# Every third weight tile's remainder computed by GpSimd in place of VectorE, in a one-core decoder layer in float32

## The chip, the cores and the metric

The kernel runs on one NeuronCore of a Trainium2 chip. Its engines work side by side and meet at semaphores: PE multiplies matrices, DVE (VectorE), ACT (ScalarE) and POOL (GpSimd) work on tiles in the on-chip memory SBUF, SP issues the loads and stores. Products land in PSUM. The metric is the device time of one execution in microseconds (us).

## The reference

One decoder layer on x of 256 tokens by 2048 channels, float32 throughout. Three sub-layers, each wrapped in two RMS norms and a shift, a scale and a gate that come from a conditioning vector c:

```python
mod = (silu(c) @ w_ada + b_ada)                      # 2048 -> 9 rows of 2048
h = rms_norm(x, g_pre) * (1 + scale) + shift
x = x + coef * gate * rms_norm(fn(h), g_post)
# fn: FFN 0, mixer, FFN 1
ffn(h) = (silu(h @ w_gate) * (h @ w_up)) @ w_down    # 2048 -> 5632 -> 2048
mixer(h): proj = h @ w_in; mLSTM heads and a spatial gate; concat @ w_out
```

Nearly all the time goes into products of 256 tokens with large weights, each of which is read from memory once.

## The kernel before, in words

A weight is taken in tiles of 256 rows by 512 columns (128 partitions x 1024 values; 410 or 412 columns in part of the mixer). For each tile, `load_w` (L271) issues a 512 KB load into one of eight `raw` buffers (`rawp`, L50), and `split_w` (L277) splits it in two: ACT casts `raw` to the rounded copy `wh` (L284), DVE subtracts, `wl = raw - wh`, the remainder (L285). Both are of the type float32r, and together they hold the weight exactly. They live in one of `NW = 4` buffers each (`wsp`, L51), or, for a few tiles kept across a sub-layer's end, in other memory ("slots"). The activations are split likewise into `hh` and `hl`, and `mm3` (L302) makes three products for each pair: hh with wh (L303), hl with wh (L304), hh with wl (L305). In part of the program the operands are swapped, and there it is L304 that takes `wl`. A tile feeds 24 matmuls of 256 columns or 12 of 512.

Beside the weight tiles run the modulation rows: `ada_sums` (L141) loads tiles of `w_ada` into the same eight `raw` buffers, and DVE adds each up with one multiply-add of 128 x 1024 values (L164, `acc`), a step after each weight tile or two. `behind` (L135) orders such an addition after the DVE remainder that was issued last (`last_split`), without a semaphore. The stages are: FFN 0's first part, in which DVE also makes the norms (to about 210 us), the rest of FFN 0 (to 800), the mixer (to 1145, with a boundary of norms to 1200), and FFN 1 (to 1890), which has few modulation rows.

The program is written through a tile framework. It gives each engine its own order of instructions, by its estimate of when each could run, and puts the semaphores in. Each engine, and SP's queue of loads, then runs strictly in that order. POOL has 40 small instructions in this kernel, among them the power -1/2 of the norms: `rstd` (L354), `brs` (L773) and `qv` (L998).

Of the kernel before, what the change touches and what calls it, by code (L numbers as in the profile page):

```python
# [8 lines left out]
F32 = mybir.dt.float32  # L9
# [23 lines left out]
def tile_layer(  # L33
# [42 lines left out]
    class Half:  # L76
        """Half of the tokens in the tile that holds the residual stream between the sub-layers"""

# [13 lines left out]

# [1 line left out]
    ident = cpool.tile([P, P], F32, name="ident")  # L94
# [7 lines left out]

# [1 line left out]
    xt = cpool.tile([P, NT, D], F32, name="xt")  # L104
# [24 lines left out]

# [1 line left out]
    last_split = [None]  # L131
    floor = [None, None]
    last_update = [None]

    def behind(ins, other):  # L135
        """ins is issued after other, on the same engine"""
        if other is not None:
            tc.add_manual_dep(ins.ins, other.ins.name, mybir.DependencyInfo(
                mybir.DependencyClass.NoSync, mybir.DependencyReason.DATA), reason="order")

    def ada_sums(runs, n):  # L141
        """Sums over the rows on each partition of the runs of n columns that start at runs; a step loads a
        tile and adds up the one before. The additions wait for the weight tile that was loaded after."""
        acc = adap.tile([P, 2, 512], F32, tag="acc", name=nm("acc"))
# [24 lines left out]
    def ada_cols(a, r, c0, n):  # L169
        """The sum over the partitions as columns of A or B."""  # L170
        sub, kind = r // 3, r % 3
        m0, m = c0 // P, n // P
        pa = ps()
        for i in range(m):
            nc.tensor.transpose(pa[:, i * P:(i + 1) * P], a[:, i * P:(i + 1) * P], ident)  # L175
        bias = v1[:, r * NK + m0:r * NK + m0 + m]
        dst = (bm if kind == 0 else am)[:, sub, m0:m0 + m]
        nc.vector.tensor_reduce(out=dst, in_=pa[:, 0:n].rearrange("p (m k) -> p m k", k=P), axis=AX.X, op=ALU.add)
        if kind == 0:
            nc.vector.tensor_tensor(out=dst, in0=dst, in1=bias, op=ALU.add)  # L180
        else:
            nc.vector.scalar_tensor_tensor(dst, dst, 1.0, bias, op0=ALU.add, op1=ALU.add)
            gp = v2[:, 16 + sub * NK + m0:16 + sub * NK + m0 + m]
            nc.vector.tensor_tensor(out=dst, in0=dst, in1=gp, op=ALU.mult)

    def ada_row(a, sub, c0):
        """The sum over the partitions as a gate's row on all of them, times g_post."""
        if gg[0] is None:
# [16 lines left out]
    def ada_unit(r, half):  # L205
        """1024 columns of one modulation row"""
        c0 = half * 1024
# [8 lines left out]
    class Side:  # L216
        """Modulation rows computed beside the weight tiles, spread evenly over n_main of them."""

# [25 lines left out]

# [1 line left out]
    pending = []  # L246
# [20 lines left out]

# [1 line left out]
    FULL = [(0, 4, 0), (4, 4, 4), (8, 4, 8), (12, 4, 12)]  # L269
# [7 lines left out]
    def split_w(rawv, slot, w):  # L277
# [6 lines left out]
        behind(nc.scalar.copy(wh, rawv), floor[1])  # L284
        last_split[0] = nc.vector.tensor_tensor(out=wl, in0=rawv, in1=wh.bitcast(F32), op=ALU.subtract)  # L285
        behind(last_split[0], floor[0])
        return wh, wl
# [19 lines left out]
    def hold(src, segs, c0, nw):  # L307
        """All the tiles of segs split and kept, those beyond the first nw halves in the large slots."""
        n = sum(nk for _, nk, _ in segs) // 2
# [3 lines left out]
    def proj_t(src, c0, segs=FULL, banks=None, first=0):  # L313
        """[512 weight columns, S] in two banks, each 2 x [128, S]: the sum over the chunks from first on."""
        banks = banks or [ps(), ps()]
# [11 lines left out]
    def proj_tok(src, c0, begun=None, w=512):  # L327
        """[S, w weight columns] in two banks, one per 128 tokens."""
        banks, done = begun or ([ps(), ps()], 0)
# [8 lines left out]

# [1 line left out]
    def parts():  # L340
        """The means of the squares over a token's quarters, the last one apart; EPS beside the others."""
        p = small((P, 8), "parts")
        nc.gpsimd.memset(p[:, 3:4], EPS)
        return p
# [12 lines left out]
    def modulate(sub, k0, nk, src, n0, n1, act):  # L357
        """h = n * A + B for the 128-channel chunks from k0 on, split into hh, hl."""
        w = n1 - n0
# [21 lines left out]
    def to_h(sub, t, q, n):  # L381
        """Four channel chunks of one half of the tokens, transposed and modulated."""
        for i in range(0, 4, 2):
# [6 lines left out]
    def pre_norm_q(sub, q, rs, act=False):  # L390
        """Four channel chunks of all the tokens."""
        modulate_q(sub, q, transposed_q(q, rs), act)
# [16 lines left out]
    def post_norm_t(y, t, r, z, last, xin):  # L409
        """x += GG * y * rstd(y) for one half of the tokens"""  # L410
        z3 = z(t)
# [18 lines left out]
    def early_w(src, c0, w):  # L430
        """The first weight tiles of the next sub-layer, split ahead into the part of hh and hl that is written
        last."""
        if src is None:
# [9 lines left out]
    def boundary(last_mm, evac, times_g, xin, y, yp, free, early, ahead, nxt, src=None, c0=None, w=512):  # L443
        """The last products of a sub-layer, one half of the tokens after the other, the residual, and the
        next sub-layer's h with the first products that take it, the first half's beside the second half's
        norms."""
        kept = [] if nxt is None else early + list(w_tiles(src, [(4, 2 * ahead, 4)], c0, w=w))
# [49 lines left out]

# [1 line left out]
    def swiglu_evac(g, gb, ub):  # L499
# [8 lines left out]
    def swiglu_sum(gb, ub, part):  # L508
        """The same after the sums over the first chunks, in part, have been added; the result takes its place."""
        pv = part.t.rearrange("p k s -> p (k s)")  # L510
# [15 lines left out]
    def swiglu_tok(g, gb, ub):  # L526
        """The same from products that have the tokens on the partitions."""
        gts = []
# [16 lines left out]
    def ffn(idx, supers, begun, xin, nxt, nxt_src=None, nxt_c0=None, nxt_w=512):  # L545
        """supers: lists of (block, chunk tiles that are left, sums over the others in SBUF or in PSUM)"""
        y = None
# [69 lines left out]

    # ================= FFN 0 =================
    # The first blocks run over the channel chunks that are modulated so far: five over the first four, three over
    # eight, and one over twelve, which stays in PSUM.  # L620
    gate_up = (w_ff_gate[0], w_ff_up[0])
    rs = [x_sumsq(t) for t in range(NT)]

    def ada_pair(c0, n):
        """A and B of the first sub-layer for n channels"""
        for acc in ada_sums((D + c0, c0), n):
# [22 lines left out]
    class First:  # L649
        """The rest of the first sub-layer's modulation beside the first weight tiles."""  # L650

# [49 lines left out]
    class Reload:  # L701
        """The residual stream again: its tile takes the products' sums."""

# [19 lines left out]

    # ================= mixer =================
    mix_side = Side([(5, 0), (5, 1), (7, 0), (7, 1)], 1)
# [27 lines left out]

    # gv, u and the gates from the last 2056 columns, gv first
    gv = Slot((P, NT, DM))
# [7 lines left out]
    def gated_norm(t):  # L763
        """layer norm of gelu(gv)"""
        st = small((P, 2, 6), "bst")
# [45 lines left out]
    def gates():  # L811
        """The stabilised gate weights: with a_s = i_s - cumsum(log f)_s and the running maximum M_l of a
        (and of the state's), pp holds exp(a_s - M_l) under the causal mask for chunk pairs (0, 0), (0, 1)
        and (1, 1); em holds exp(-m_l)."""
        nc.vector.scalar_tensor_tensor(ea, gx[:, :, 4:8], -1.0, gx[:, :, 4:8], op0=ALU.mult, op1=ALU.max)
# [72 lines left out]
    def spatial():  # L888
        """z = gelu(u) * (W v + b), into the second half of the concatenation"""
        for i in range(2):  # L890
# [76 lines left out]

    # o: sigmoid, times the head norm's weight
    so = Slot((P, NT, DM))
# [8 lines left out]
    def values():  # L978
        """The weighted sums of the values, and of ones beside them."""
        for h in range(H):  # L980
# [91 lines left out]

    # ================= FFN 1 =================
    side[0] = Side([(8, i) for i in range(2)], 100)
# [31 lines left out]
```

## Time and profile before

| | |
|---|---|
| runs | 1909.9 and 1910.4 us, median 1910.15 |
| profiled execution | span 1910.4 us, which is its time; nothing of note lies around the span |
| PE matmul | 1862.1 us busy, 97% |
| DVE | 1356.0 us, 71% |
| ACT | 855.2 us, 45% |
| POOL | 17.2 us, 1% |
| loads | 500 MB, 262 GB/s on average, 334 GB/s from 40 to 210 us |

Busy times of PE are modelled ends of pipelined matmuls, so a full row says that PE always had work, and no more. The stages differ: a share over the whole span says little about one of them, so the rows further down are taken by stage. A wait row names an engine, what it waited for, the time in total, how often and the longest.

### The profile page before, as it was taken

What the parts mean: (1) busy time and instruction counts of PE and PEld (TensorE: products, weight loads), DVE (VectorE), ACT (ScalarE), POOL (GpSimd) and SP (SyncE); (2) the same over time, 40 slices, a digit from 0 to 9 for tenths busy, and PEclk for the clock granted to TensorE, in tenths of its full rate; (3) what the DMA queues carried; (4) which work ended last, traced back from release to release, by engine and by line L of the source; (5) the groups of instructions that cost most, each with busy time, mean ns of one, the idle gap of its engine ahead of it and who ended that gap; (6) DMA issues with size and microseconds to landing.
All of it is one profiled execution on the core that took longest, in us unless ns stands there. A gap on an engine that the chain in (4) does not pass through costs nothing.

```text
span 1910.4 us, 30740 instructions
## 1 busy us (share of the span) xinstructions
PE 1862.1 (97%) x12357; PEld 1714.0 (90%) x12357; DVE 1356.0 (71%) x1465; ACT 855.2 (45%) x1059; POOL 17.2 (1%) x40
## 2 busy tenths in 40 slices
PE   3999999999999999999999999999999999999998
PEld 2999998899988998799988887999889999899986
DVE  7788788778887878868888986555556555555455
ACT  3545444444443434555545446444444444334443
POOL 0000000000000000000000000000000000000000
PEclk9999999999999999999999999999999999999999
DMA  9999889888898998678688994666666666666552
GB/s 352 344 329 333 285 300 317 303 304 309 299 326 305 357 310 298 207 220 278 230 278 308 354 326 129 217 218 211 227 221 209 220 218 212 220 225 214 187 187 88
DMA packets 232647, 500.31 MB, mean 262 GB/s; under 512 B 16829, under 2 KB 28333, under 8 KB 231993
## 3 DMA queue, kind: packets, MB, share of 16 engines
q1 hardware_dynamic: 232504, 498.36, 76.7%
q8 instruction: 96, 1.57, 0.3%
q14 instruction: 47, 0.38, 0.1%
HBM read 496.19 MB, written 2.10 MB: 261 GB/s over the span
## 4 chain that ended last, share of the span: by engine, by line
PE 89%; issue 8%; DVE 2%; ACT 1%; POOL 1%; DMA 0%; POOLq 0%; DVEq 0%; ACTq 0%
PE ps L303 29%; PE ps L305 29%; PE ps L304 29%; DVE acc L164 1%; PE ps L175 0%; DMA xt<-in_x_dram 0%; PE ps L403 0%; POOL rstd L354 0%; DVE wl L285 0%; ACT t L365 0%; DMA raw<-in_w_in_dram 0%; PE ps L895 0%; ACT t L348 0%; POOL brs L773 0%; ACT hh L336 0%
## 5 line engine op out<-in xcount | busy, mean ns | idle before, releaser
L285 DVE TENSOR_TENSOR wl<-raw,wh 128x1024 fp32r<-128x1024 f32 (+2 forms) x637 | 769.0, 1210 | 488.7 <-ACT wh L284 488.0
L284 ACT CAST wh<-raw 128x1024 fp32r<-128x1024 f32 (+2 forms) x637 | 661.2, 1042 | 882.6 <-PE ps L304 453.5
L303 PE MATMUL ps<-hh,wh 128*128 128x256 f32 x2816 | 794.5, 282 | 3.7 <-ACT hh L336 3.1
L304 PE MATMUL ps<-hl,wh 128*128 128x256 f32 x2816 | 792.2, 281 | 0.0
L305 PE MATMUL ps<-hh,wl 128*128 128x256 f32 x2816 | 791.6, 281 | 0.0
L303 PEld LDWEIGHTS ps<-hh,wh 128*128 128x128 f32 x2816 | 531.7, 189 | 5.4 <-ACT hh L336 3.7
L304 PEld LDWEIGHTS ps<-hl,wh 128*128 128x128 f32 x2816 | 531.9, 189 | 1.1 <-issue 0.5
L305 PEld LDWEIGHTS ps<-hh,wl 128*128 128x128 f32 x2816 | 531.4, 189 | 0.1
L164 DVE SCALAR_TENSOR_TENSOR acc<-raw,cs,acc 128x1024 f32<-128x1024 f32 x270 | 345.1, 1278 | 0.5
L303 PE MATMUL ps<-wh,big 128*128 128x512 f32 x804 | 318.0, 395 | 0.0
L305 PE MATMUL ps<-wh,big 128*128 128x512 f32 x804 | 316.4, 394 | 0.0
L304 PE MATMUL ps<-wl,big 128*128 128x512 f32 x804 | 316.4, 393 | 0.0
L305 PEld LDWEIGHTS ps<-wh,big 128*128 128x128 f32 x804 | 150.9, 188 | 35.8
L303 PEld LDWEIGHTS ps<-wh,big 128*128 128x128 f32 x804 | 151.0, 188 | 34.4
L304 PEld LDWEIGHTS ps<-wl,big 128*128 128x128 f32 x804 | 151.0, 188 | 34.3
L303 PE MATMUL ps<-wh,hh 128*128 128x512 f32 (+2 forms) x336 | 127.2, 380 | 0.0
L304 PE MATMUL ps<-wl,hh 128*128 128x512 f32 (+2 forms) x336 | 126.0, 375 | 0.6 <-DVE wl L285 0.6
L305 PE MATMUL ps<-wh,hl 128*128 128x512 f32 (+2 forms) x336 | 125.7, 374 | 0.0
L304 PEld LDWEIGHTS ps<-wl,hh 128*128 128x128 f32 x336 | 63.2, 188 | 9.3 <-DVE wl L285 1.3
L305 PEld LDWEIGHTS ps<-wh,hl 128*128 128x128 f32 x336 | 63.1, 188 | 8.4
L303 PEld LDWEIGHTS ps<-wh,hh 128*128 128x128 f32 x336 | 63.0, 188 | 8.0 <-ACT hh L336 0.2
L645 ACT COPY big<-ps 128x512 f32<-128x512 f32 x32 | 18.8, 588 | 45.0 <-PE ps L305 43.4
(195 smaller groups left out, 718.2 us busy)
## 6 DMA issues: line engine op xcount, KB each, us to landing
raw<-in_w_ada_dram SPq DMA_DIRECT2D x224, 512.0 KB
raw<-in_w_ff_gate_dram SPq DMA_DIRECT2D x176, 512.0 KB
raw<-in_w_ff_up_dram SPq DMA_DIRECT2D x176, 512.0 KB
raw<-in_w_ff_down_dram SPq DMA_DIRECT2D x176, 512.0 KB
raw<-in_w_ada_dram SPq DMA_DIRECT2D x128, 256.0 KB
raw<-in_w_in_dram SPq DMA_DIRECT2D x48, 512.0 KB
raw<-in_w_out_dram SPq DMA_DIRECT2D x32, 512.0 KB
raw<-in_w_in_dram SPq DMA_DIRECT2D x24, 412.0 KB
```

The costliest lines, as they stand in the source:

```text
L164: ins = nc.vector.scalar_tensor_tensor(a, raw[:, j, :, :], cs[:, k:k + 1], a, op0=ALU.mult, op1=ALU.add)
L284: behind(nc.scalar.copy(wh, rawv), floor[1])
L285: last_split[0] = nc.vector.tensor_tensor(out=wl, in0=rawv, in1=wh.bitcast(F32), op=ALU.subtract)
L303: nc.tensor.matmul(o, lh, rh, start=start, stop=False, skip_group_check=True)
L304: nc.tensor.matmul(o, lh, rl, start=False, stop=False, skip_group_check=True)
L305: nc.tensor.matmul(o, ll, rh, start=False, stop=stop, skip_group_check=True)
L645: nc.scalar.copy(part.t.rearrange("p k s -> p (k s)")[:, u * 1024 + i * 512:u * 1024 + (i + 1) * 512], banks[i])
```

## The change

A counter goes up with each weight tile. At every third count, if the tile lives in the four `wsp` buffers, POOL computes `wl` with the same operation, and `last_split` stays at the DVE remainder before it; the order behind `floor[0]`, which places some remainders after a norm's instruction, isn't set for these either. All else in the diff takes out comments and docstrings, so that lines of the changed file from split_w on stand five further down.

```diff
+    n_split = [0]
...
         behind(nc.scalar.copy(wh, rawv), floor[1])
-        last_split[0] = nc.vector.tensor_tensor(out=wl, in0=rawv, in1=wh.bitcast(F32), op=ALU.subtract)
-        behind(last_split[0], floor[0])
+        n_split[0] += 1
+        if slot is None and n_split[0] % 3 == 0:
+            nc.gpsimd.tensor_tensor(out=wl, in0=rawv, in1=wh.bitcast(F32), op=ALU.subtract)
+        else:
+            last_split[0] = nc.vector.tensor_tensor(out=wl, in0=rawv, in1=wh.bitcast(F32), op=ALU.subtract)
+            behind(last_split[0], floor[0])
         return wh, wl
```

213 remainders move to POOL, of 648. PE's and SP's orders stay nearly as they were; DVE's and POOL's change. Two places are shown. The numbers in the names are the tiles' own, the same before and after.

The first place is DVE at the start of the third modulation pass in FFN 0 (145 to 160 us in the trace of before). Before:

```order
L285 TENSOR_TENSOR wl_1647<-raw_1644,wh_1646 128x1024
L164 SCALAR_TENSOR_TENSOR acc_1602<-raw_1641,cs,acc_1602 128x1024
L337 TENSOR_TENSOR hl<-t_237_1592,hh 128x512
L378 TENSOR_SCALAR t_336_2387<-xt,rstd_125 128x512
L378 TENSOR_SCALAR t_337_2389<-xt,rstd_139 128x512
L285 TENSOR_TENSOR wl_1682<-raw_1679,wh_1681 128x1024
L337 TENSOR_TENSOR hl<-t_238_1597,hh 128x512
L164 SCALAR_TENSOR_TENSOR acc_1602<-raw_1676,cs,acc_1602 128x1024
L285 TENSOR_TENSOR wl_1716<-raw_1713,wh_1715 128x1024
L285 TENSOR_TENSOR wl_1746<-raw_1743,wh_1745 128x1024
```

And now, on the same engine:

```order
L290 TENSOR_TENSOR wl_1647<-raw_1644,wh_1646 128x1024
L165 SCALAR_TENSOR_TENSOR acc_1602<-raw_1641,cs,acc_1602 128x1024
L342 TENSOR_TENSOR hl<-t_237_1592,hh 128x512
L165 SCALAR_TENSOR_TENSOR acc_1602<-raw_1676,cs,acc_1602 128x1024
L342 TENSOR_TENSOR hl<-t_238_1597,hh 128x512
L383 TENSOR_SCALAR t_336_2387<-xt,rstd_125 128x512
L383 TENSOR_SCALAR t_337_2389<-xt,rstd_139 128x512
L290 TENSOR_TENSOR wl_1716<-raw_1713,wh_1715 128x1024
L290 TENSOR_TENSOR wl_1746<-raw_1743,wh_1745 128x1024
```

`wl_1682` has left DVE for POOL, and the addition that stood behind it has moved ahead of a norm's two instructions.

The second place is POOL in the mixer at 1024 us, where `qv` is the power that the head norm needs. Before, nothing but that stood on POOL between 928 and 1143 us. Now:

```order
L288 TENSOR_TENSOR wl_10478<-raw_10475,wh_10477 128x1024
L288 TENSOR_TENSOR wl_10569<-raw_10566,wh_10568 128x1024
L288 TENSOR_TENSOR wl_10639<-raw_10636,wh_10638 128x1024
L1003 TENSOR_TENSOR qv<-qv,nhalf 128x8
L288 TENSOR_TENSOR wl_10724<-raw_10721,wh_10723 128x1024
L288 TENSOR_TENSOR wl_10788<-raw_10785,wh_10787 128x1024
```

`qv` stands behind `wl_10639` in POOL's queue, a tile whose DVE remainder stood behind `fac<-qv,rec` before.

## Rows read from the trace of the kernel before

**Rows 1.** The page, parts 1 and 2: busy time of the engines, and DVE's busy tenths in 40 slices of the span.

```profile
PE 1862.1 (97%) x12357; PEld 1714.0 (90%) x12357; DVE 1356.0 (71%) x1465; ACT 855.2 (45%) x1059; POOL 17.2 (1%) x40
...
DVE  7788788778887878868888986555556555555455
```

**Rows 2.** Busy time by stretch of the program: the stretch, its length, then the busy us (and instructions) of each engine, PE's granted clock, the share of the DMA engines and GB/s.

```profile
40.00:210.00 170.00, 170.00 (x1421) 169.85 (x1420) 133.85 (x128) 81.23 (x102) 0.00 (x0) 1.00 0.96 334
210.00:500.00 290.00, 289.34 (x2072) 270.98 (x2072) 234.87 (x241) 129.77 (x144) 0.00 (x0) 1.00 0.87 300
500.00:800.00 300.00, 300.00 (x1890) 270.26 (x1889) 242.14 (x251) 128.20 (x148) 1.29 (x4) 1.00 0.88 306
800.00:1050.00 250.00, 246.48 (x1386) 223.46 (x1385) 204.79 (x289) 134.75 (x208) 9.57 (x12) 1.00 0.78 258
1050.00:1145.00 95.00, 95.00 (x427) 77.17 (x426) 84.33 (x95) 43.03 (x56) 0.65 (x2) 1.00 0.95 340
1145.00:1200.00 55.00, 52.66 (x234) 41.91 (x233) 36.91 (x61) 32.94 (x60) 1.94 (x6) 0.97 0.46 151
1200.00:1890.00 690.00, 690.00 (x4866) 646.18 (x4865) 383.21 (x355) 289.97 (x311) 0.00 (x0) 1.00 0.64 207
```

**Rows 3.** The page, part 4: the chain that ended last, by engine.

```profile
PE 89%; issue 8%; DVE 2%; ACT 1%; POOL 1%; DMA 0%; POOLq 0%; DVEq 0%; ACTq 0%
```

**Rows 4.** The group of the remainders on DVE in six stretches, in this order: 40 to 210, 210 to 500, 500 to 800, 800 to 1050, 1050 to 1145 and 1200 to 1890 us. Count, busy us and mean ns of one, then idle time before them and what ended it.

```profile
L285 DVE TENSOR_TENSOR wl<-raw,wh 128x1024 fp32r<-128x1024 f32 x61 | 74.0, 1222 | 33.6 <-ACT wh L284 33.5
...
L285 DVE TENSOR_TENSOR wl<-raw,wh 128x1024 fp32r<-128x1024 f32 x101 | 123.0, 1223 | 50.6 <-ACT wh L284 50.6
...
L285 DVE TENSOR_TENSOR wl<-raw,wh 128x1024 fp32r<-128x1024 f32 (+1 forms) x102 | 124.1, 1218 | 47.7 <-ACT wh L284 47.7
...
L285 DVE TENSOR_TENSOR wl<-raw,wh 128x1024 fp32r<-128x1024 f32 (+2 forms) x85 | 95.6, 1129 | 34.4 <-ACT wh L284 34.2
...
L285 DVE TENSOR_TENSOR wl<-raw,wh 128x1024 fp32r<-128x1024 f32 x31 | 37.5, 1216 | 6.0 <-ACT wh L284 6.0
...
L285 DVE TENSOR_TENSOR wl<-raw,wh 128x1024 fp32r<-128x1024 f32 x244 | 299.0, 1226 | 303.6 <-ACT wh L284 303.3 <-DMA t<-in_g_post_dram 0.3
```

**Rows 5.** POOL's instructions in order of time: start us, duration us, engine, line, operation, what is written and read.

```profile
1.18 0.29 POOL masks.py:199 TENSOR_SCALAR_AFFINE_SELECT ident<-ident 128x128 f32<-128x128 f32 x1
...
865.47 1.25 POOL L773 TENSOR_TENSOR brs<-bve,nhalf 128x1 f32<-128x1 f32 x1 [39.86 <-DVE bve L771]
...
916.00 1.18 POOL L856 TENSOR_SCALAR_AFFINE_SELECT t<-t 128x512 f32<-128x512 f32 x1 [43.17 <-DVE t L851]
927.95 0.63 POOL L856 TENSOR_SCALAR_AFFINE_SELECT t<-t 128x512 f32<-128x512 f32 x1 [10.77 <-ACT big L868]
...
1149.69 0.55 POOL L354 TENSOR_TENSOR rstd<-parts,nhalf 128x1 f32<-128x1 f32 x1 [1.45 <-DVE parts L352]
```

**Rows 6.** DVE's instructions at the same moments, in order of time, the same columns.

```profile
802.11 0.16 DVE L352 TENSOR_TENSOR parts<-parts 128x1 f32<-128x1 f32 x1 [0.21 <-ACT t L348]
...
865.31 1.00 DVE L285 TENSOR_TENSOR wl<-raw,wh 128x824 fp32r<-128x824 f32 x1
...
916.00 0.68 DVE L863 TENSOR_TENSOR t<-t,t 128x512 f32<-128x512 f32 x1
...
928.10 1.03 DVE L863 TENSOR_TENSOR t<-t,t 128x512 f32<-128x512 f32 x1
```

**Rows 7.** Waits over the span: who waited for what, us in total, times, the longest. The last row is of SP's queue of loads.

```profile
ACT wh L284 <- PE ps L304: 453.5, 264, 4.4
...
ACT wh L284 <- PE ps L305: 343.8, 210, 2.4
...
SPq L273 <- DVE wl L285: 907.6, 458, 21.7
```

**Rows 8.** Busy time by stretch again, one stretch of 50 us inside FFN 0; columns as in rows 2.

```profile
450.00:500.00 50.00, 50.00 (x425) 50.00 (x424) 42.83 (x44) 22.50 (x25) 0.00 (x0) 1.00 0.88 305
```

**Rows 9.** Order of time on ACT, DVE and PE around tile 1682 (151 to 153 us), then ACT and PE around tile 11440 (1124 to 1128 us): the cast, the remainder, the first matmul that takes it.

```profile
150.71 1.05 ACT L284 CAST wh<-raw 128x1024 fp32r<-128x1024 f32 x1
...
151.92 1.23 DVE L285 TENSOR_TENSOR wl<-raw,wh 128x1024 fp32r<-128x1024 f32 x1
...
153.20 0.39 PE L305 MATMUL ps<-hh,wl 128*128 128x256 f32 x1
...
1124.50 1.04 ACT L284 CAST wh<-raw 128x1024 fp32r<-128x1024 f32 x1
...
1127.44 0.39 PE L304 MATMUL ps<-wl,big 128*128 128x512 f32 x1
```

**Rows 10.** Order of time on POOL, ACT, DVE and PE around `qv`: the power, the cast of tile 10639, the product that waits for the power, the remainder of tile 10669, and the first matmul that takes that remainder.

```profile
1024.12 2.01 POOL L998 TENSOR_TENSOR qv<-qv,nhalf 128x8 f32<-128x8 f32 x1 [95.54 <-DVE qv L997]
...
1023.36 1.05 ACT L284 CAST wh<-raw 128x1024 fp32r<-128x1024 f32 x1 [1.42 <-PE ps L305]
...
1026.17 0.17 DVE L999 TENSOR_TENSOR fac<-qv,rec 128x8 f32<-128x8 f32 x1 [1.54 <-POOL qv L998]
...
1028.66 1.22 DVE L285 TENSOR_TENSOR wl<-raw,wh 128x1024 fp32r<-128x1024 f32 x1
...
1034.60 0.40 PE L304 MATMUL ps<-wl,hh 128*128 128x512 f32 x1
```

## The prediction, made before the changed kernel ran

> **What bounds the kernel now.** Read first the busy times and the slices [rows 1]: PE is busy 97% of the span; DVE 71%, but it is at 6 to 9 tenths in the first 25 of the 40 slices (to 25 x 47.8 = 1194 us) and at 4 to 6 behind them. A mean over two such parts says little, so read next the busy time by stretch [rows 2]. In every stretch PE has work nearly all the time. What it lacks is 290.00 - 289.34 = 0.7 us, 250.00 - 246.48 = 3.5 us and 55.00 - 52.66 = 2.3 us, 6.5 us in all between 40 and 1890 us. The chain that ended last says the same [rows 3]: 89% of it is PE, DVE is 2%. So DVE's remainders are work beside PE, and a lighter DVE can win little: 6.5 us if every wait of PE in the middle went away. The start and the tail have no moved remainder on their path.
>
> Then ask how late a remainder may come. ACT's cast waits for PE to give up a buffer, 264 + 210 times, 453.5 + 343.8 us [rows 7]: with four buffers, it runs when PE goes on to the next tile and still has three in hand. PE does 425 matmuls in 50 us [rows 8], 24 to a tile, so a tile takes 50 x 24 / 425 = 2.82 us; three are 8.5 us, less the cast's 1.05 us [rows 9] leaves about 7.4 us for a remainder that takes 1.22 us on DVE [rows 4].
>
> **What the change removes.** A third of the remainders leave DVE. By the counts of the six stretches [rows 4] these are 20, 34, 34, 28, 10 and 81 at 1.22, 1.22, 1.22, 1.13, 1.22 and 1.23 us, so DVE's busy time of [rows 2] falls to 133.9 - 24.4 = 109.5, 234.9 - 41.5 = 193.4, 242.1 - 41.5 = 200.6, 204.8 - 31.6 = 173.2, 84.3 - 12.2 = 72.1 and 383.2 - 99.6 = 283.6 us. Taken alone this is worth nothing to PE, by the first paragraph.
>
> **What it adds: a price that no row shows.** The trace has no subtraction of 128 x 1024 on POOL. From below: POOL's select with one input takes 0.29 us for 128 values a partition and, undisturbed, 0.63 us for 512 [rows 5], so 0.89 ns a value and 0.18 us fixed; 1024 values are 1.09 us. A second input can't make it cheaper. From above: the smallest two-input instruction takes 0.55 us on POOL [rows 5] and 0.16 us on DVE [rows 6], 3.4 times as long; 3.4 x 1.22 = 4.2 us. I take 2.0 us: the fixed 0.18 and twice 0.91, a read of each input in turn, since the select is plain arithmetic over long rows as the subtraction is, and the small one is a power.
>
> The GPSIMD Engine Reference of the Trainium skill (Elementwise, side by side) puts a two-input operation at about 2.6 cycles a value at 1.2 GHz, an estimate of 2.2 us here; with it the fullest stretch below would go from 97% to 99%, and the time by under 2 us. The same page's Engine selection advises against GpSimd for such work.
>
> **What it blocks.** POOL and DVE are not independent here. At 865.47 a power of one value takes 1.25 us instead of 0.55; it ends 0.41 us behind the DVE remainder that ran from 865.31 to 866.31. At 916.00 a select takes 1.18 us instead of 0.63 beside a DVE instruction with two inputs. And it goes the other way: at 928.10 the same DVE instruction takes 1.03 us instead of 0.68, and it ends 0.54 us behind POOL's select, which held until 928.58 [rows 5, 6]. So I add POOL's time to DVE's as if both were one engine, for an upper bound of the load; DVE's instructions that read PSUM are counted too, though none is shown to be held up.
>
> The load with POOL at 2.0 us: 109.5 + 40 = 149.5 of 170 us; 193.4 + 68 = 261.4 of 290; 200.6 + 68 = 268.6 of 300; 173.2 + 56 = 229.2 of 250; 72.1 + 20 = 92.1 of 95; 283.6 + 162 = 445.6 of 690. All fit, and the queues that this makes (a wait for one DVE instruction of up to 1.28 us, then 2.0) are hidden by the 7.4 us. If that cover is gone, each us of lateness is one of PE.
>
> **Where the cover is thin.** Tile 1682 is cast by 151.76 and taken by PE at 153.20 [rows 9]; POOL can end at 151.76 + 2.0 = 153.8 at the earliest, and at 155.1 behind a full DVE instruction: 0.6 to 1.9 us late, I take 1.2. Tile 11440 is cast by 1125.54 and taken at 1127.44: 0.1 to 1.4, I take 0.7. The others have over 4 us. For the stretch that is full to 97% I take 1 us.
>
> **The queue that `qv` now shares.** `qv` stands behind tile 10639, cast by 1024.41 [rows 10]; that remainder ends near 1026.6, the power (about 1.5 us without the DVE instruction beside it) near 1028.1, where it ended at 1026.13. DVE waits for it in `fac`, and behind that stands the remainder of tile 10669, which ran from 1028.66 to 1029.88. As 10639 is no longer ahead of it, it comes at about 1028.4; PE takes it at 1034.60. Nothing is late. The powers at the sub-layers' ends stand behind remainders cast several us before; hidden too.
>
> **The raw buffers.** A moved tile's buffer comes free 0.8 us later, up to 2.1 with the wait, and SP's loads behind it with it. Already SP waits 458 times, 907.6 us, for a remainder [rows 7], while PE stays full; hidden by the loads in flight, zero. If that cover is gone, see the third rival.
>
> **The sum.** 1910.4 us of the profiled execution + 1.2 + 0.7 + 1 = 1913.3. The median of the runs is 1910.15, 0.25 less, so I predict **1913**. At the low price of 1.09 us the three terms vanish and the time is 1910, less what DVE's relief may give.
>
> **Rivals.** First, on the other side: POOL is dearer, and the two engines that share their way become the bound up to 1145 us. The stretches are full at (170 - 109.5) / 20 = 3.0 us, then 2.8, 2.9, 2.7 and 2.3 us a remainder. At 3.3 us they are over by 5 + 16 + 13 + 16 + 10 = 60 us: 1970. At the upper bound of 4.2 us, 23 + 46 + 43 + 41 + 19 = 172 us: 2082. The 2% (38 us) are reached at about 3.1 us. For it: the price is unseen, the margins are thin, both directions of blocking are in the trace. Against: select's slope, and that reads of PSUM need not wait. FFN 1, at 65%, would not feel it in any case. Chance 0.18.
>
> Second, DVE's relief wins back the 6.5 us that PE lacks in the middle: 1904. For it: DVE is on the chain there [rows 3]. Against: these places are norms at sub-layers' ends, with few remainders. Chance 0.07.
>
> Third, the later buffers starve the loads from 40 to 210 us, where the DMA engines are busy to 0.96 [rows 2]: 20 x 2.1 = 42 us at most, 1952. Against: PE is full there, and so are the DMA engines, so loads are waiting in line. Chance 0.04.
>
> The change can't fail to do what it says: the remainders stand on POOL in the new order.
>
> **Chances and range.** The forecast has 0.71. Slower by over 2% (above 1948; 2% is about what a measurement of this kernel can tell from no change): most of the first rival, 0.17, half of the third, 0.02, so 0.19. Faster by over 2% would need PE not to be the bound: 0.01. Within: 0.80. The range goes from 1904 (the second rival) to 1952 (the third, and the lower edge of the first), and leaves out about 0.16 above and 0.03 below.
>
> **What would show it.** In the profile after, POOL's remainder at about 2.0 us undisturbed and longer beside DVE, DVE's additions with means above 1.28 us, DVE and POOL together under the length of each stretch, and PE still full. If the mean on POOL is over 3 us and PE waits for `wl` all through FFN 0, the first rival holds, and FFN 1's stretch should then have kept its length. If SP or ACT wait for loads from 40 to 210 us and PE thins out there alone, it is the third. The forecast fails with a PE that waits for remainders at many places.

## The result, and the profile after

The changed kernel takes 1927.57 us (1926.91 and 1928.23), the kernel before 1910.15: a ratio of 1.0087, 95% interval 1.007 to 1.0103. That lies within 2% and inside the predicted range, on the side of slower, but it is 17 us where the forecast's sum had 3. The profiled execution has a span of 1926.5 us, 16.1 more than before.

First the page of the kernel after, parts 1 and 4 and three of the groups of part 5 (busy us, mean ns of one, idle time before them and what ended it).

```profile
PE 1866.3 (97%) x12357; PEld 1714.3 (89%) x12357; DVE 1241.0 (64%) x1252; ACT 856.3 (44%) x1059; POOL 561.1 (29%) x253
...
PE 85%; DVE 7%; issue 4%; DMA 2%; ACT 1%; POOL 1%; SPq 0%; DVEq 0%; POOLq 0%; ACTq 0%
...
L288 POOL TENSOR_TENSOR wl<-raw,wh 128x1024 fp32r<-128x1024 f32 (+2 forms) x213 | 544.1, 2555 | 1286.9 <-ACT wh L285 1215.5
L290 DVE TENSOR_TENSOR wl<-raw,wh 128x1024 fp32r<-128x1024 f32 (+2 forms) x424 | 538.6, 1272 | 574.1 <-ACT wh L285 573.5
L165 DVE SCALAR_TENSOR_TENSOR acc<-raw,cs,acc 128x1024 f32<-128x1024 f32 x270 | 395.3, 1464 | 1.6
```

213 remainders have moved. PE has as much work as before and still fills 97%; DVE's share of the chain that ended last went from 2% [rows 3] to 7%. DVE lost a third of its remainders, yet its busy time fell only from 1356.0 [rows 1] to 1241.0 us: its instructions got longer.

Next the busy time by stretch after the change; columns as in [rows 2]: the stretch, its length, busy us (and count) of PE, PEld, DVE, ACT, POOL, the granted clock, the DMA share, GB/s.

```profile
40.00:210.00 170.00, 168.60 (x1411) 168.29 (x1410) 137.67 (x108) 81.74 (x102) 55.32 (x20) 1.00 0.95 332
210.00:500.00 290.00, 288.54 (x2066) 270.07 (x2065) 226.08 (x207) 128.41 (x142) 87.12 (x33) 1.00 0.87 296
500.00:800.00 300.00, 299.29 (x1894) 269.77 (x1894) 220.74 (x213) 128.57 (x146) 90.12 (x37) 1.00 0.89 310
800.00:1050.00 250.00, 240.87 (x1346) 218.78 (x1345) 183.87 (x254) 131.74 (x208) 73.49 (x41) 0.99 0.74 242
1050.00:1145.00 95.00, 91.70 (x403) 72.78 (x402) 89.52 (x77) 39.50 (x51) 34.29 (x11) 1.00 0.92 328
...
1215.00:1905.00 690.00, 690.00 (x4866) 646.18 (x4865) 301.28 (x272) 291.12 (x313) 196.07 (x82) 1.00 0.66 208
```

Between 40 and 1145 us PE lacks 1105 - 1089.00 = 16.0 us; before, the same five stretches of time lacked 4.2 [rows 2]. The two stretches of the mixer (800 to 1145) hold 9.13 + 3.30 = 12.4 us of it, where they lacked 3.5 before. FFN 1, with few modulation rows, kept its 690 us full.

What PE waited for `wl`, from the waits of the kernel after, then of the kernel before (total, times, longest):

```profile
PE ps L309 <- DVE wl L290: 3.6, 4, 1.3
PE ps L309 <- POOL wl L288: 3.3, 3, 1.6
...
PE ps L310 <- DVE wl L290: 2.9, 1, 2.9
...
PE ps L310 <- POOL wl L288: 1.4, 1, 1.4
```

```profile
PE ps L304 <- DVE wl L285: 0.6, 2, 0.4
```

That is 11.2 us in nine waits for remainders, against 0.6 us in two before. **More than half of it, 6.5 us, is for remainders that stayed on DVE**, 4.7 us for moved ones. The other part is the granted clock. The longest wait ends at 945.72; in its last part the clock goes to half, and it stays there behind the wait. Three stretches of PE around it (stretch, length, PE busy, clock, DMA share, GB/s), and one of the kernel before:

```profile
943.00:946.00 3.00, 0.28 (x1) 0.84 0.00 0
946.00:951.00 5.00, 5.00 (x24) 0.50 0.89 264
951.00:952.00 1.00, 1.00 (x8) 0.58 0.95 348
```

```profile
1150.00:1155.00 5.00, 4.43 (x12) 0.66 0.00 0
```

From these, 1.2 in place of 2.4 GHz lasts 0.48 / 0.5 + 5 + 0.42 / 0.5 = 6.8 us, from 945.04 to 951.84. PE works in 6.1 us of it, from 945.72 on, and loses half of them, 3.1 us. Before, between 40 and 1890 us, there was one such stretch, worked out likewise as 0.34 x 5 / 0.5 = 3.4 us long, which is gone in this profile. So of 16.1 us, 10.6 are new waits for `wl` and 3.1 - 1.7 = 1.4 the clock; small waits for `hh`, `t` and `hl` grew by some 1.6, and about 2.5 are not assigned.

The place of the longest wait, in order of time on POOL, DVE and PE:

```profile
942.24 2.35 POOL L288 TENSOR_TENSOR wl<-raw,wh 128x1024 fp32r<-128x1024 f32 x1 [6.32 <-PE ps L310]
...
942.48 3.19 DVE L290 TENSOR_TENSOR wl<-raw,wh 128x1024 fp32r<-128x1024 f32 x1
...
945.72 0.58 PE L310 MATMUL ps<-hh,wl 128*128 128x256 f32 x1 [2.86 <-DVE wl L290]
```

POOL starts on the remainder of `wl_9867`, the counter's 318th tile, which PE needs only at 956.05. 0.24 us later DVE starts on a remainder of its own that PE needs at once, and it ends 1.08 us after POOL's: 3.19 us in place of 1.22. The moved tile had over 11 us to spare; the one that stayed did not.

The four smaller waits for a remainder on DVE are of two kinds. At 789.70 and 876.74 the remainder itself was held: 2.91 us, and 2.67 for one of 824 values that otherwise takes 1.01. At 882.79 and 886.62, 1.3 us each, it took its usual 1.0 us and came late, in DVE's order behind instructions that were held. The remainder of 876.74, that of 882.79, and the addition that stands ahead of the one of 886.62:

```profile
874.02 2.67 DVE L290 TENSOR_TENSOR wl<-raw,wh 128x824 fp32r<-128x824 f32 x1
...
881.73 1.01 DVE L290 TENSOR_TENSOR wl<-raw,wh 128x824 fp32r<-128x824 f32 x1
882.65 2.98 DVE L165 SCALAR_TENSOR_TENSOR acc<-raw,cs,acc 128x1024 f32<-128x1024 f32 x1
```

At another place the delay goes in part by a buffer. Near the mixer's end, in order of time on POOL, DVE, SP's queue, ACT and PE, and then the waits of SP's loads of weights for DVE's additions, first from 1085 to 1118 us before and then from 1100 to 1135 after:

```profile
1121.73 2.56 POOL L288 TENSOR_TENSOR wl<-raw,wh 128x1024 fp32r<-128x1024 f32 x1 [6.61 <-ACT wh L285]
...
1121.92 4.77 DVE L165 SCALAR_TENSOR_TENSOR acc<-raw,cs,acc 128x1024 f32<-128x1024 f32 x2
...
1125.39 0.37 SPq L274 DMA_DIRECT2D raw<-in_w_out_dram  x1
...
1130.69 1.05 ACT L285 CAST wh<-raw 128x1024 fp32r<-128x1024 f32 x1 [3.84 <-DMA raw<-in_w_out_dram]
...
1131.88 3.02 POOL L288 TENSOR_TENSOR wl<-raw,wh 128x1024 fp32r<-128x1024 f32 x1 [7.59 <-ACT wh L285]
...
1134.95 0.50 PE L309 MATMUL ps<-wl,big 128*128 128x512 f32 x1 [1.17 <-POOL wl L288]
```

```profile
SPq L273 <- DVE acc L164: 7.5, 9, 0.8
```

```profile
SPq L274 <- DVE acc L165: 10.2, 10, 3.0
```

A remainder on POOL holds up an addition, the addition gives its `raw` buffer back late, the next load of a weight is issued late, its cast waits 3.84 us for it, and that tile's remainder, on POOL too, is 1.17 us late for PE. That remainder is held as well, 3.02 us in place of 2.40, so about half of the 1.17 us is the buffer's. This is read from one place of the trace; no run isolates it.

### The profile page after: what moved, and what is told of

It is laid out like the page before. It is cut to its first block, busy times and chain, and to the rows that moved or that the text cites. A ratio compares the mean times of both kernels' runs of the same rounds, so it can differ in the third digit from the quotient of the medians.

```text
span 1926.5 us, 30882 instructions
## 1 busy us (share of the span) xinstructions
PE 1866.3 (97%) x12357; PEld 1714.3 (89%) x12357; DVE 1241.0 (64%) x1252; ACT 856.3 (44%) x1059; POOL 561.1 (29%) x253
## 4 chain that ended last, share of the span: by engine, by line
PE 85%; DVE 7%; issue 4%; DMA 2%; ACT 1%; POOL 1%; SPq 0%; DVEq 0%; POOLq 0%; ACTq 0%
PE ps L310 28%; PE ps L309 28%; PE ps L308 28%; DVE acc L165 3%; DVE wl L290 2%; DMA raw<-in_w_out_dram 1%; ACT wh L285 1%; POOL wl L288 1%; DMA raw<-in_w_in_dram 0%; PE ps L176 0%; ACT t L370 0%; DMA xt<-in_x_dram 0%; DMA raw<-in_w_ff_down_dram 0%; DMA raw<-in_w_ada_dram 0%; DMA raw<-in_w_ff_gate_dram 0%
## 5 line engine op out<-in xcount | busy, mean ns | idle before, releaser
L288 POOL TENSOR_TENSOR wl<-raw,wh 128x1024 fp32r<-128x1024 f32 (+2 forms) x213 | 544.1, 2555 | 1286.9 <-ACT wh L285 1215.5
L290 DVE TENSOR_TENSOR wl<-raw,wh 128x1024 fp32r<-128x1024 f32 (+2 forms) x424 | 538.6, 1272 | 574.1 <-ACT wh L285 573.5
L165 DVE SCALAR_TENSOR_TENSOR acc<-raw,cs,acc 128x1024 f32<-128x1024 f32 x270 | 395.3, 1464 | 1.6
```

Of the source, the lines that this page charges most:

```text
L165: ins = nc.vector.scalar_tensor_tensor(a, raw[:, j, :, :], cs[:, k:k + 1], a, op0=ALU.mult, op1=ALU.add)
L288: nc.gpsimd.tensor_tensor(out=wl, in0=rawv, in1=wh.bitcast(F32), op=ALU.subtract)
```

## The experiments

Each ratio is to the kernel before on the same chip, where that took 1910.6 us (the first four versions), 1910.7 (the next three) or 1912.0 (the last three). Three theories: **held up** (or sharing): POOL's two-input instruction keeps a two-input DVE instruction from running, and the other way round, and time is lost where PE, or a buffer, waits for the one that is held. **Late**: a moved tile itself comes late, since POOL takes longer. **Order**: the new order of DVE's and ACT's instructions is worse by itself. Later a fourth, **load**: what counts is the sum of both engines' times.

**One stage at a time.** The change in FFN 0 alone, in the mixer alone, in FFN 1 alone (`on[0]` is true in that stage only):

```diff
-        if slot is None and n_split[0] % 3 == 0:
+        if slot is None and n_split[0] % 3 == 0 and on[0]:
```

> Every third remainder goes to GpSimd in FFN 0 alone (to about 800 us). Sharing theory (GpSimd's remainder of 2.4 us and DVE's two-input instructions exclude each other, and this costs only where DVE is on PE's path): the steps seen in the changed kernel up to 806 us, 3 us in all, so about 1913 us. Order theory (DVE's new order of instructions costs, wherever it is): the same share of the program as of the loss, 42% of 16.5 us, so about 1917.

> Every third remainder goes to GpSimd in the mixer alone (800 to 1200 us). Sharing theory: most of the loss, 13 us, so about 1923 us, with PE waiting for a DVE remainder near 940 us and the granted clock at half for some us behind it. Order theory: 21% of 16.5 us, about 1914.

> Every third remainder goes to GpSimd in FFN 1 alone (from 1200 us), where DVE is busy 55% of the time. Sharing theory: no cost, 1910 us, within 2. Order theory: 37% of 16.5 us, about 1916.

FFN 0: 1913.69 us, ratio 1.0013 (1.0004 to 1.0021), and PE waits once for a POOL remainder, 1.4 us. Mixer: 1922.01 us, 1.0051 (1.0038 to 1.0063). FFN 1: 1911.04 us, 0.9999 (0.999 to 1.0008). So 213 moved remainders do not cost alike: 86 of them, in FFN 1, cost nothing; 39, in the mixer, cost some 10 us. In the mixer's run PE has the same wait of 2.9 us, but the clock stayed at 1.00 behind it, so that part of the expectation was a miss. The wait, and the stretches of PE around its end at 942.23:

```profile
PE ps L311 <- DVE wl L291: 2.9, 1, 2.9
```

```profile
940.00:943.00 3.00, 0.77 (x6) 1.00 0.00 0
943.00:946.00 3.00, 3.00 (x28) 1.00 0.91 262
```

The three costs add up to some 12 us, where the whole change costs 17. The 3.1 us of half clock are in none of the three profiles; the rest of the difference is not explained.

**The order alone.** The changed program, but DVE computes the third remainder too, without the order behind the norms:

```diff
-            nc.gpsimd.tensor_tensor(out=wl, in0=rawv, in1=wh.bitcast(F32), op=ALU.subtract)
+            nc.vector.tensor_tensor(out=wl, in0=rawv, in1=wh.bitcast(F32), op=ALU.subtract)
```

> The change with all remainders on DVE: every third is issued on DVE again, but isn't noted as the last remainder and isn't placed behind the floor, so that additions may stand ahead of it as in the changed kernel. Sharing theory: 1910 us, within 2. Order theory: about 1926.

1910.97 us, ratio 0.9999 (0.999 to 1.0008). So this order costs nothing. It is not quite the change's: in the two traces DVE's other instructions follow each other differently at some 70 places, so the order theory is settled only by the next version. The group of the 213 remainders also tells what DVE was relieved of:

```profile
L288 DVE TENSOR_TENSOR wl<-raw,wh 128x1024 fp32r<-128x1024 f32 (+2 forms) x213 | 257.6, 1209 | 118.1 <-ACT wh L285 114.2
```

257.6 us left DVE, but its busy time fell by 115.0: 142.6 us came back, 395.3 - 345.1 = 50.2 of them as longer additions. In the next version, where POOL reads nothing, only 1118.3 - (1356.0 - 257.6) = 19.9 come back.

**The relief alone.** POOL fills those `wl` with zeros, so it writes, but reads nothing; a third of the remainders is left out of the products:

```diff
-            nc.gpsimd.tensor_tensor(out=wl, in0=rawv, in1=wh.bitcast(F32), op=ALU.subtract)
+            nc.gpsimd.memset(wl.bitcast(F32), 0.0)
```

> The third remainder is left out: GpSimd sets its tile to zero (it reads nothing, and waits for no cast), so the output lacks that part. DVE is relieved as in the change. Sharing theory: DVE isn't held up by an instruction that only writes, so its additions keep 1.28 us, and the loss is gone: 1904 to 1910 us. Order theory: about 1926. Late theory (only the moved tiles themselves come too late from GpSimd): 1904 to 1910 too.

1911.78 us, ratio 1.0005 (0.9996 to 1.0014). Moved instructions aside, all of DVE's, ACT's and POOL's instructions follow each other in this trace as in the change's, but for one `fac` on DVE. So **the order theory falls**: the same order without POOL's reads loses nothing. A DVE that is 257.6 us lighter wins nothing either. And POOL's writes do not hold the additions: their mean is 1279 ns, as before. This version's busy times and additions, then the additions before:

```profile
PE 1861.4 (97%) x12357; PEld 1714.4 (90%) x12357; DVE 1118.3 (59%) x1252; ACT 855.6 (45%) x1059; POOL 219.3 (11%) x253
...
L165 DVE SCALAR_TENSOR_TENSOR acc<-raw,cs,acc 128x1024 f32<-128x1024 f32 x270 | 345.4, 1279 | 1.6
```

```profile
L164 DVE SCALAR_TENSOR_TENSOR acc<-raw,cs,acc 128x1024 f32<-128x1024 f32 x270 | 345.1, 1278 | 0.5
```

Not every DVE instruction is spared by a write: five of the 24 `t<-xt,rstd`, an instruction with one tile as its input, take 1.0 to 1.3 us beside a memset and 0.48 otherwise.

**The same load on DVE.** The third remainder stays on DVE and is computed twice there, 2 x 1.21 us, about what POOL takes:

```diff
+        if slot is None and n_split[0] % 3 == 0:
+            behind(nc.vector.tensor_tensor(out=wl, in0=rawv, in1=wh.bitcast(F32), op=ALU.subtract), floor[0])
         last_split[0] = nc.vector.tensor_tensor(out=wl, in0=rawv, in1=wh.bitcast(F32), op=ALU.subtract)
```

> The kernel before, with every third remainder computed twice on DVE (2.44 us in place of 1.22), nothing on GpSimd. Sharing theory: two engines that exclude each other are one engine with the sum of the load, and the sum is nearly that of the changed kernel (1.22 + 1.22 here, 2.4 there), so 1920 to 1930 us, the loss at the same places. If the loss comes from something else on GpSimd (its queue, its latency): about 1912.

1938.32 us, ratio 1.0144 (1.0128 to 1.0159), outside what was expected. PE waits 13.5 us in ten waits at one line alone, up to 4.7 us. One engine that does both is slower here than two that exclude each other. That POOL can use the time in which DVE waits or reads PSUM would explain it, but the run doesn't show it: PE's order differs in places in this version, and its granted clock averages 0.993 over the span, the change's 0.997, which makes an estimate of up to 0.004 x 1938 = 8 us. So the 11 us between it and the change are no price.

**Half of the remainders.** `% 2` in place of `% 3`:

```diff
-        if slot is None and n_split[0] % 3 == 0:
+        if slot is None and n_split[0] % 2 == 0:
```

> Every second remainder goes to GpSimd. Sharing theory: DVE and GpSimd together come to 169 of 170, 294 of 290, 302 of 300, 254 of 250 and 102 of 95 us in the stretches of before up to 1145 us, so FFN 0's steady part is full for the first time and the time is about 1945 us. Late theory: half as many more late tiles, about 1934.

1955.26 us, ratio 1.0228 (1.0214 to 1.0242). 318 moved remainders in place of 213 cost 43 us in place of 17. Part of that is the clock: it averages 0.991 over the span, where the change has 0.997 and the kernel before 0.998, an estimate of up to 0.007 x 1954 = 14 us of the 43. The first stretch of FFN 0, and the groups of POOL's remainders and DVE's additions:

```profile
40.00:210.00 170.00, 163.06 (x1337) 161.84 (x1338) 142.81 (x96) 79.08 (x100) 77.28 (x27) 0.99 0.91 310
```

```profile
L288 POOL TENSOR_TENSOR wl<-raw,wh 128x1024 fp32r<-128x1024 f32 (+2 forms) x318 | 818.1, 2573 | 1045.2 <-ACT wh L285 1009.4
...
L165 DVE SCALAR_TENSOR_TENSOR acc<-raw,cs,acc 128x1024 f32<-128x1024 f32 x270 | 455.9, 1689 | 2.0
```

POOL's price is the same, but the additions went from 1464 to 1689 ns, and FFN 0 now loses more: PE lacks 6.9 us from 40 to 210 us, 1.4 in the change. This is the first rival's place, reached by the count and not by the price.

**All but one.** The remainder of `wl_9867` alone goes back to DVE; the other 212 stay moved:

```diff
-        if slot is None and n_split[0] % 3 == 0:
+        if slot is None and n_split[0] % 3 == 0 and n_split[0] != 318:
```

> The change, but one moved remainder, that of wl_9867 at 942 us, stays on VectorE. PE needed it only at 956.05, 11.5 us after its cast, so it cannot itself have been late. Held-up theory (GpSimd's 2.4 us keep a VectorE remainder that PE waits for from running): PE's wait of 2.86 us at 945 goes, and the half clock behind it with it; the step of 5.9 us there falls to under 1, and the time is 1921 to 1923 us. Lateness theory (moved tiles come late by GpSimd's longer time): that tile had spare time, so nothing changes, 1927 us. Load theory (the sum of both engines' times is what counts): 1 remainder of 213, under 0.2 us, 1927 us.

1922.38 us, ratio 1.0057 (1.0043 to 1.0071): from 1.0087 down by 0.0030, 5.7 us, for one instruction of 213 that was itself 11 us early. The two 95% intervals just touch, so the size is better taken from the trace: 2.0 us less of one wait and 3.1 us of half clock. The same stretches of PE, and the remainder that was held:

```profile
943.00:946.00 3.00, 2.12 (x18) 1.00 0.29 40
946.00:951.00 5.00, 5.00 (x46) 1.00 0.92 291
```

```profile
942.95 1.21 DVE L290 TENSOR_TENSOR wl<-raw,wh 128x1024 fp32r<-128x1024 f32 x1
```

The wait of 2.86 us is down to 0.9 and the half clock is gone; the order of all other instructions is the change's. Lateness and load can't do this; the held-up theory gave 1921 to 1923. What is left to lateness are the 4.7 us of waits for moved tiles, and in part these were held too (2.74, 5.77 and 3.02 us in place of 2.40).

**Only that one.** The kernel before, with the 318th remainder alone on POOL:

```diff
-        last_split[0] = nc.vector.tensor_tensor(out=wl, in0=rawv, in1=wh.bitcast(F32), op=ALU.subtract)
-        behind(last_split[0], floor[0])
+        n_split[0] += 1
+        if slot is None and n_split[0] == 318:
+            nc.gpsimd.tensor_tensor(out=wl, in0=rawv, in1=wh.bitcast(F32), op=ALU.subtract)
+        else:
+            last_split[0] = nc.vector.tensor_tensor(out=wl, in0=rawv, in1=wh.bitcast(F32), op=ALU.subtract)
+            behind(last_split[0], floor[0])
```

> The kernel before, with only the remainder of wl_9867 on GpSimd. Held-up theory: PE's wait for VectorE's next remainder appears as far as the lead there, under 1 us before the change, does not cover 2.4 us: 1911 to 1914 us, the upper end if the clock falls behind the wait; if VectorE is not yet behind at this place without the other moved tiles, 1910.5. Lateness and load theories: 1910.5 us, no change.

1910.72 us, ratio 0.9997 (0.9989 to 1.0006). The hold is there all the same, both ways, in order of time on POOL and DVE:

```profile
934.45 3.47 POOL L288 TENSOR_TENSOR wl<-raw,wh 128x1024 fp32r<-128x1024 f32 x1 [5.72 <-ACT wh L285]
...
934.45 1.21 DVE L290 TENSOR_TENSOR wl<-raw,wh 128x1024 fp32r<-128x1024 f32 x1
935.58 0.47 DVE L927 SCALAR_TENSOR_TENSOR big<-ps,v,big 128x254 f32<-128x254 f32 x1
935.98 3.04 DVE L290 TENSOR_TENSOR wl<-raw,wh 128x1024 fp32r<-128x1024 f32 x1
```

POOL's takes 3.47 us behind DVE's first, then DVE's second takes 3.04 behind POOL's. But here DVE is not yet late: the first of the two remainders is done at 935.66, and PE takes it at 936.54. In the change, DVE came to the same remainder only 0.38 us before PE did. So no wait of PE is added, and the hold costs nothing. It takes the lateness that the other moved tiles leave on DVE before a single one decides.

**Shorter holds.** POOL computes each moved remainder as two instructions of 512 values:

```diff
-            nc.gpsimd.tensor_tensor(out=wl, in0=rawv, in1=wh.bitcast(F32), op=ALU.subtract)
+            for j in range(2):
+                nc.gpsimd.tensor_tensor(
+                    out=wl[:, j, :], in0=rawv[:, j, :], in1=wh[:, j, :].bitcast(F32), op=ALU.subtract)
```

> The change, but GpSimd takes each moved remainder as two instructions of 512 values, one behind the other. Held-up theory: a VectorE instruction can get in between, so the longest hold falls from 2.4 to about 1.3 us, which the leads of up to 0.9 us and a VectorE instruction's own slack cover far better: 1915 to 1921 us. Lateness and load theories: each moved remainder takes GpSimd as long or 0.2 us longer, 213 x 0.2 = 43 us more of load: 1927 to 1932 us.

1922.55 us, ratio 1.0057 (1.0045 to 1.007): 5.7 us better than the change, but 1.5 above the expected 1915 to 1921. The order of DVE's, ACT's and POOL's instructions is the change's. POOL's remainders, DVE's additions, and a wait of PE:

```profile
L289 POOL TENSOR_TENSOR wl<-raw,wh 128x512 fp32r<-128x512 f32 (+2 forms) x426 | 620.3, 1477 | 1210.9 <-ACT wh L285 1028.6
...
L165 DVE SCALAR_TENSOR_TENSOR acc<-raw,cs,acc 128x1024 f32<-128x1024 f32 x270 | 376.0, 1392 | 1.6
```

```profile
PE ps L312 <- DVE wl L292: 2.2, 2, 1.8
```

POOL is busy 76 us more than in the change, 620.3 against 544.1, and the program is faster: that speaks against load and against lateness, and for the length of one hold. The additions are shorter, 1392 ns in the mean against 1464, and PE's wait behind the 318th tile is 1.8 us in place of 2.86. How much of the 5.7 us is the half clock behind 945 us, which this version does not have, and how much the shorter holds elsewhere, it does not tell apart; the version with one tile put back gains as much.

None of these versions beats the kernel before; the memset version puts the relief that one could win at zero.

## Why the prediction was right, and where its sum was not

**PE bounds the kernel, and DVE's relief is worth nothing.** Right: the memset version is as slow as the kernel before. With it falls the second rival (1904 us).

**The price on POOL, 2.0 us.** Too low: undisturbed it is about 2.4 us. One row has the shortest, the median and the longest of the 213 (ns):

```profile
L288 POOL TENSOR_TENSOR wl<-raw,wh x213: 1953/2402/5774, 39.5 to 1900.1; 128x1024 fp32r<-128x1024 f32 x101, 128x824 fp32r<-128x824 f32 x4, 128x820 fp32r<-128x820 f32 x2
```

It lay inside the bounds of 1.09 and 4.2 us, and far from the 3.1 us at which the first rival would pass 2%. The select, from which 2.0 was scaled, was the wrong relative. The Trainium skill's GPSIMD Engine Reference (Elementwise, side by side) had it: about 2.6 cycles a value at 1.2 GHz, an estimate of 2.2 us without the fixed part; the median of 2.40 less the 0.18 fixed us of the select is 2.22, so the trace agrees.

**The two engines' times add up, and every stretch fits.** As an upper bound of the load that held where the loss was small. At 2.4 us the stretches would hold 157.5 of 170, 275.0 of 290, 282.2 of 300, 240.4 of 250, 96.1 of 95 and 478.0 of 690 us: only the one near the mixer's end is over, by 1. PE lost 3.3 us there and 9.1 in the stretch that was full to 96%, so the load was near the edge. But the one-tile and the half-tile versions show that the sum is not what sets the loss. The sign that the prediction names for it, DVE and POOL together under the length of each stretch, can't be read from the profile: a held instruction counts as busy, so from 40 to 210 us the two have 137.67 + 55.32 = 193.0 of 170 us, while PE lacks 1.4.

**"These queues are hidden by the 7.4 us" and "the others have over 4 us": this step failed.** The 7.4 us are what a tile has that is cast early and computed at once. I went through the moved tiles for their spare time and not through the remainders that stay on DVE. POOL holds up those, or a DVE instruction ahead of them, by up to 2.2 us at a time in the rows below, and in places, most of them in the mixer, they had little lead. Of 11.2 us of waits for `wl`, 6.5 are for such tiles, and the longest brings the half clock with it. The queue for the moved tiles was too short as well: one DVE instruction of up to 1.28 us and then 2.0 make 3.3 us, but POOL can stand behind several, and the longest took 5.77 us, for which PE waits 1.63. The two thin places that I did name were right: tile 1682 was forecast 1.2 us late and PE waits 1.40; for tile 11440, 0.7 and 0.50. For the stretch from 1050 to 1145 us I took 1 beside that 0.7, and PE lacks 3.3 there; for that from 800 to 1050 I took nothing, and PE lacks 9.1 in place of 3.5.

**`qv` is hidden.** Right that PE does not wait for it. It starts at 1039.51 behind a moved remainder, but POOL has been idle for 0.30 us by then: its input on DVE was held by that remainder (the first row of the last section).

**"Raw buffers: hidden, zero."** Right for FFN 0's first part: PE lacks 1.4 us from 40 to 210 us, and that is tile 1682; so the third rival falls there. Not right near the mixer's end, where a late buffer is part of a wait of 1.17 us.

**The clock was not in the sum at all.** With a wait of 2.86 us came 6.8 us at half the clock, 3.1 us more.

So the forecast's case, a small loss, came true, with the mechanism that the prediction had read from the trace; the sum had 1.2 + 0.7 + 1 = 2.9 us where 16 belong, mainly for want of a check on the tiles that did not move. That the range of 1904 to 1952 held 1927.57 owes more to its width than to the sum. The sign of failing that the prediction names, a PE that waits for remainders at many places, came about in small: nine waits in place of two. And a measurement can tell far less than 2% here, as the interval of 1.007 to 1.0103 shows. The first rival's sign was right for the mixer, and FFN 1 kept its length as it would have it, but its price was not reached.

## What to carry to other kernels

When work moves to an engine that shares a way to memory with the one relieved, look at the work that stays: each of its instructions that needs that way can now be held for the whole length of the moved one, so it needs that much lead, wherever it is. Here FFN 1, where the relieved engine has slack, took 86 moved remainders for nothing; so place moved work there and keep it from the places where PE takes a result within a microsecond of its making. And the relief of an engine that the busiest one hardly waits for was worth nothing here, so there was no gain to set against it.

## What was unexpected of the hardware

The hold strikes small instructions as hard as large ones. Two rows of DVE after the change, of 8 values and of 4, and one of POOL:

```profile
1036.87 2.36 DVE L1001 TENSOR_TENSOR qv<-qv,rec 128x8 f32<-128x8 f32 x1
...
1112.76 2.38 DVE L185 TENSOR_TENSOR am<-am,v 128x4 f32<-128x4 f32 x1
...
1048.79 9.11 POOL L288 TENSOR_TENSOR wl<-raw,wh 128x1024 fp32r<-128x1024 f32 x2 [7.25 <-ACT wh L285]
```

The two of DVE take some 0.16 us otherwise. POOL in turn can be kept out for long by DVE instructions that follow each other closely: the two remainders from 1048.79 on take 9.11 us together, the first of them the longest of all, 5.77 us, and PE waits 1.63 us for it. The Trainium skill's SBUF — State Buffer (Who interferes with whom) tells of an exclusive lock of the shared ports, held for a whole instruction, against a DVE instruction with two inputs in SBUF only if POOL reads; these rows and the memset version's additions agree.

DVE's instructions that read PSUM go on beside POOL: in the version with one moved tile, one of them at 935.58, while POOL's remainder runs, takes its usual 0.47 us. In the change, ten of the `big<-big,ps` lie wholly inside a remainder of POOL's and take 0.69 us, as the six others do. The sum of both engines' loads, which counts these instructions too, is then too high.

The half clock does not follow each such wait: 2.86 us in the change's profile brought it, 2.9 us in that of the mixer alone did not. Why is not shown.
